# Moving GpSimd's arithmetic to VectorE and building RWKV's chunk inverses from 16x16 blocks

## The chip, the core and the metric

The kernel runs on one core of a Trainium2 chip. The core has a matrix engine (TensorE, PE in the profile, with its weight loads as PEld), a vector engine (VectorE, DVE), a scalar engine (ScalarE, ACT), a general engine (GpSimd, POOL) and a queue that issues transfers (SyncE, SP). Each engine executes its instructions strictly in the order in which they were placed in its stream; an instruction whose semaphores are not set holds up everything behind it on that engine. The metric is device time in microseconds of one launch.

## The reference

Two layers of a decoder over 512 tokens of 1024 channels. Each layer:

```python
h = modulate(rms_norm(x, norm1_g), shift1, scale1)
p = h @ w_in                      # columns for three mixers
y_ret, y_rwkv, y_conv = retention(p_ret), rwkv7_time_mix(p_rwkv), short_conv(p_conv)
merged = sum_i sigmoid(h @ w_gate + b_gate)_i * (y_i @ w_branch[i])
x = x + gate1 * (merged @ w_o)
h2 = modulate(rms_norm(x, norm2_g), shift2, scale2)
x = x + gate2 * hier_moe(h2)      # top-1 of 4 groups, then top-2 of its 8 experts
```

The part that matters most here is RWKV's recurrence, over 8 heads of 64:

```python
sk = einsum('bhvk,bhk->bhv', state, kht)
state = state * wt - sk[..., None] * (at * kht) + vt[..., None] * ktt
y = einsum('bhvk,bhk->bhv', state, rt)
```

## The kernel before

**Precision.** Projections are computed in float32 from fp32r parts. `split` (L216, L217) makes of a tile a high part on ScalarE and a low part, source minus high part, on VectorE or on the engine that the caller names. `wsplit` (L330) loads a weight block of 128 columns (`raw`) and splits it into `whi` and `wlo`, two buffers each; `mm3` (L345) then runs 24 matmuls per block: for each of 8 row blocks, `hTh` with `whi`, `hTl` with `whi` and `hTh` with `wlo`. In retention (`ret`), convolution (`conv`), part of the first norm and the first gates the caller names GpSimd for the low part. Five kinds of elementwise operation of the mixers are on GpSimd too, and so are the running sum of `merge` (L939) and the low parts of the routed tokens (L1048).

**Order.** The program is written as generators for RWKV, retention and convolution; a static scheduler interleaves them and fixes each engine's stream before the launch. RWKV runs in two halves (`rwkv_half`, two blocks of 128 channels, four heads each). Between its steps, projections of the other mixers stand on TensorE; retention's head norm (`head_norm`, with `rsqrt`, L206 to L211, and L582) gives `rB`, which L564 transposes; RWKV's gives `YN` for L884, and its key norm gives `rsq_y`, on which L701's matmul rests.

**The chunk inverse.** A chunk has 64 steps, and its state update needs the inverse of a 64x64 unit triangular matrix for each pair of head and chunk, 32 pairs in a half; even and odd chunks (`par`) lie on different halves of the partitions. `Lt` holds the strict parts, made on VectorE behind matmuls (L735, L739), and L764 uses them first. Each matrix has two diagonal 32x32 blocks (`ab`), so a half has 64 blocks of 32x32. Stores (L774) put them into DRAM (`nd`), and a load (L780) returns them with one block per partition (`P`). On VectorE, 31 steps of two operations (L786: outer product of a column of `P` with the rows found so far; L788: add into `T`) solve all 64 blocks at once on 64 partitions. `T` and its transpose go to DRAM (`td`, `ttd`) and come back into `tts`, which holds the transposed inverses in place, and `TA` (named `Ei` in the profile, whose buffer it uses). Then TensorE makes the off-diagonal 32x32 block: L806 multiplies the off-diagonal part of `Lt` with `TA`, ScalarE copies it (`Pb`, named `a`), and L811 multiplies with `tts`; ScalarE writes the result into `tts` (L813). This is done for the chunks of one parity and then for those of the other, 16 matmuls each time. L820 and what follows use `tts`.

**Routing.** After the second norm, tokens `x` are scaled by `r`. ScalarE makes `xr` (L1046) and the high part `xh` (L1047), GpSimd the low part of the first 768 channels (L1048); the last 256 channels' low parts (L1084) are made on VectorE in `late_xl`, behind the slot masks `oh` (L1080) of the first group in the program text. `route` finds groups and experts on VectorE (L1173 to L1195), counts places with matmuls (L1198, L1200), and L1203 makes the positions `pos`. `gather` multiplies `xh` and `xl` with `oh` (L1254), alternating between them over the four token blocks.

Of the kernel before, what the change touches and what calls it, by code (L numbers as in the profile page):

```python
# [37 lines left out]
def _consts():  # L38
# [136 lines left out]
class Kern:  # L175
# [44 lines left out]
    def setup(self):  # L220
# [139 lines left out]
    def norm1(self, l):  # L360
# [8 lines left out]
        if l == 0:  # L369
# [4 lines left out]
            ws = [self.wsplit(w_in(at), 8, nc.gpsimd if i % 2 else None, (self.wp, np_)[i // 2])  # L374
# [71 lines left out]
    def dense(self, l):  # L446
# [35 lines left out]
        self.merge(l, mg, [self.gate(l, mg, d, i, nc.gpsimd) for d, i in MERGE[:5]])  # L482
# [6 lines left out]
    def ret(self, l, pool, between):  # L489
        nc, c = self.nc, self.c  # L490
        b2 = lambda tag: pool.tile([128, S], F32, tag=tag, name=tag)
        def blk(o, h):
            ps = next(self.proj(l, "w_in", o * MW + h * 128, 1, nc.gpsimd))
            return ps

        A, B, C, Dt, E, F, G, H = "rA rB rC rD rE rF rG rH".split()
        for h in range(4):
            qk = []
            for o, tag in ((0, A), (1, B)):
# [7 lines left out]
                nc.gpsimd.tensor_tensor(t, t, self.sinT, op=OP.mult)  # L507
# [12 lines left out]
            nc.gpsimd.tensor_tensor(ch(qd), ch(q), c("decq")[:, None, h * 128:(h + 1) * 128].to_broadcast([128, 4, 128]),  # L520
# [121 lines left out]
    def rwkv_half(self, l, hf, rw, b2, half, wal, gl, wa, gd):  # L642
# [14 lines left out]
        for b in range(2):  # L657
# [30 lines left out]
            nc.gpsimd.tensor_scalar(a, a, 0.5, 0.5, op0=OP.mult, op1=OP.add)  # L688
# [81 lines left out]
        for par in range(2):  # L770
            for ab in range(2):
# [718 lines left out]
```

## Time and profile before

| what | us |
|---|---|
| plain runs, median of 3 | 2608.41 (2608.26 to 2610.09) |
| profiled execution | 2605.45, its span 2603.7 |
| mean granted TensorE clock | 0.966 of full |
| GpSimd: low parts of weights (L217) | 70 instructions, 170.2 |
| GpSimd: sums of the merge (L939) | 32, 53.4 |
| GpSimd: rotary products (L507) | 16, 21.9 |
| GpSimd: low parts of tokens (L1048) | 8, 14.8 |
| VectorE: inverse steps (L786, L788) | 248, 141.1 |

The times of one layer's stages, layer 0: first norm to 60 us, mixers 60 to 500, merge to 685, output projection and routing to 760, experts to 1300. Layer 1 follows the same pattern some 1304 us later.

How to read the rows: a timeline row gives start, duration, engine, line, operation, output and inputs by the program's names, and in brackets the idle time before it and what ended it. A row of waits gives engine, tile and line that waited, what it waited for, and then microseconds in total, number of times, longest. A row of groups gives the shapes and count, the busy time and the mean in ns, and the idle time before.

### The profile page before, as it was taken

Reading aid. Unit: us, or ns where it says so; the run is one execution under the profiler, and the core shown is the slowest. Engines: PE = TensorE matmul, PEld = TensorE weight load, DVE = VectorE, ACT = ScalarE, POOL = GpSimd, SP = SyncE. Lnnn points to the kernel's source line nnn. Section 1 sums busy time; section 2 is a strip of 40 time slices with the busy share of each in tenths; the row PEclk is TensorE's granted clock in tenths of the full one; section 3 lists DMA queues with packets and bytes.
Section 4 is the critical chain, followed back from the end, with each engine's and each line's share of the span. In section 5 each row is a group of like instructions: output and inputs, shape, how many; then the busy total and the mean of one; then the engine's idle time right before and its main releaser. Section 6 shows DMA issues by size and latency. Waiting matters only on the chain. (4 is left out here: it accounts for less than half of the span.)

```text
span 2603.7 us, 33403 instructions
## 1 busy us (share of the span) xinstructions
PE 2336.9 (90%) x13262; PEld 1559.8 (60%) x13262; DVE 1219.7 (47%) x2505; ACT 658.9 (25%) x1122; POOL 330.1 (13%) x200
## 2 busy tenths in 40 slices
PE   5988979899979999899989889798999799999997
PEld 4666667777854444444456666677789544444443
DVE  7677767676442223122246776676734422221223
ACT  4322323222331111111143222232233311111111
POOL 2132223211010000000011223232110100000000
PEclk9999989999989999999999999899999899999999
DMA  7131124575629997799842321255736299889993
GB/s 281 62 85 66 41 81 167 193 262 192 245 86 411 388 379 281 288 421 382 354 151 69 83 67 42 80 185 185 247 97 243 103 416 386 331 340 421 420 382 149
DMA packets 136610, 589.80 MB, mean 227 GB/s; under 512 B 34820, under 2 KB 35588, under 8 KB 87300
## 3 DMA queue, kind: packets, MB, share of 16 engines
q1 hardware_dynamic: 133280, 579.19, 58.7%
q10 hardware_dynamic: 3172, 8.45, 1.0%
q8 instruction: 106, 1.74, 0.3%
q14 instruction: 52, 0.43, 0.0%
HBM read 569.76 MB, written 13.63 MB: 224 GB/s over the span
## 5 line engine op out<-in xcount | busy, mean ns | idle before, releaser
L1273 PE MATMUL ps_mm<-w_at,xg_at 128*64 128x512 f32 x2048 | 470.4, 595 | 0.0
L345 PE MATMUL ps_mm<-hTh_at,wlo_at 128*128 128x512 f32 x1024 | 412.8, 403 | 38.3 <-POOL wlo_at L217 26.3
L345 PE MATMUL ps_mm<-hTh_at,whi_at 128*128 128x512 f32 x1024 | 414.8, 405 | 3.0 <-DVE wa_at L613 2.4
L345 PE MATMUL ps_mm<-hTl_at,whi_at 128*128 128x512 f32 x1024 | 410.8, 401 | 0.0
L1273 PEld LDWEIGHTS ps_mm<-w_at,xg_at 128*64 128x64 f32 x2048 | 155.6, 137 | 263.3 <-issue 258.3
L216 ACT ACTIVATE whi_at<-raw_at 128x1024 fp32r<-128x1024 f32 (+1 forms) x180 | 169.6, 944 | 449.1 <-PE ps_mm L345 303.3
L1305 PE MATMUL ps_rt<-w_at,hT_at 128*64 128x512 f32 x1024 | 268.3, 598 | 0.0
L1277 DVE TENSOR_TENSOR h_at<-h_at,ps_mm 128x256 f32<-128x256 f32 x65 | 27.4, 421 | 482.9 <-ACT h_at L1276 482.9
L345 PEld LDWEIGHTS ps_mm<-hTh_at,wlo_at 128*128 128x128 f32 x1024 | 197.0, 192 | 92.7 <-POOL wlo_at L217 29.7
L345 PEld LDWEIGHTS ps_mm<-hTh_at,whi_at 128*128 128x128 f32 x1024 | 197.1, 193 | 50.8 <-issue 7.6
L345 PEld LDWEIGHTS ps_mm<-hTl_at,whi_at 128*128 128x128 f32 x1024 | 197.1, 192 | 43.3 <-issue 3.2
L217 POOL TENSOR_TENSOR wlo_at<-raw_at,whi_at 128x1024 fp32r<-128x1024 f32 x70 | 170.2, 2435 | 391.2 <-ACT whi_at L216 339.4
L1305 PEld LDWEIGHTS ps_rt<-w_at,hT_at 128*64 128x64 f32 x1024 | 86.2, 136 | 136.4 <-issue 134.3
L217 DVE TENSOR_TENSOR wlo_at<-raw_at,whi_at 128x1024 fp32r<-128x1024 f32 (+1 forms) x110 | 115.4, 1050 | 105.8 <-ACT whi_at L216 105.5
L1311 DVE SCALAR_TENSOR_TENSOR ps_rt<-ps_rt,ws_at,g2b_at 128x512 f32<-128x512 f32 x66 | 50.1, 759 | 215.8 <-PE ps_rt L1305 212.6
L1254 PE MATMUL ps_sm<-oh_at,xh_at 128*128 128x256 f32 x512 | 131.4, 295 | 6.3 <-DVE oh_at L1080 2.4
L1276 ACT ACTIVATE h_at<-ps_mm 128x256 f32<-128x256 f32 x65 | 24.9, 383 | 440.6 <-PE ps_mm L1273 440.6
L1254 PE MATMUL ps_sm<-oh_at,xl_at 128*128 128x256 f32 x512 | 127.8, 289 | 0.0
L311 DVE SCALAR_TENSOR_TENSOR w_ada_at<-w_ada_at,crow_at 128x1024 f32<-128x1024 f32 x80 | 100.9, 1262 | 41.4 <-DMA w_ada_at<-in_w_ada_dram 41.2
L1329 DVE TENSOR_TENSOR x_at<-x_at,ps_sm 128x512 f32<-128x512 f32 x136 | 91.7, 687 | 55.1 <-PE ps_sm L1326 54.7
L1254 PEld LDWEIGHTS ps_sm<-oh_at,xh_at 128*128 128x128 f32 x512 | 100.3, 196 | 25.2 <-issue 25.2
L1326 PE MATMUL ps_sm<-yh_at,ohT_at 128*128 128x512 f32 x264 | 107.2, 410 | 5.2 <-ACT yh_at L1312 3.5
(364 smaller groups left out, 3404.3 us busy)
## 6 DMA issues: line engine op xcount, KB each, us to landing
w_at<-in_w_exp_dram SPq DMA_DIRECT2D x384, 1024.0 KB, 9.6
raw_at<-in_w_in_dram SPq DMA_DIRECT2D x84, 512.0 KB, 3.6
w_ada_at<-in_w_ada_dram SPq DMA_DIRECT2D x80, 512.0 KB, 4.3
raw_at<-in_w_gate_dram SPq DMA_DIRECT2D x48, 512.0 KB, 4.1
raw_at<-in_w_branch_dram SPq DMA_DIRECT2D x48, 256.0 KB, 3.9
w_ada_at<-in_w_ada_dram SPq DMA_DIRECT2D x8, 1024.0 KB, 12.8
raw_at<-in_w_o_dram SPq DMA_DIRECT2D x16, 512.0 KB, 4.4
yin_at<-yd SPq DMA_DIRECT2D x24, 256.0 KB, 3.3
```

The costliest lines, as they stand in the source:

```text
L216: nc.scalar.activation(hi, src, AF.Copy)
L217: (eng or nc.vector).tensor_tensor(lo, src, hi.bitcast(F32), op=OP.subtract)
L311: nc.vector.scalar_tensor_tensor(w, w, 1.0, self.crow, op0=OP.mult, op1=OP.mult, accum_out=m)
L345: self.nc.tensor.matmul(ps, w[a][:, k], x[b][:, k], start=n == 0, stop=n == last)
L1254: nc.tensor.matmul(po if len(oh.shape) == 4 else pg, src[:, t, k * 128:(k + 1) * 128], oh[:, t], start=i == 0, stop=i == 7)
L1273: nc.tensor.matmul(ph[64 * j:64 * j + 64].rearrange("p (u f) -> p u f", u=2), xg(k), wgu(k)[:, :, 256 * j:256 * j + 256], start=k == 0, st ...
L1276: nc.scalar.activation(h, ph[:, :256], AF.Silu)
L1277: nc.vector.tensor_tensor(h, h, ph[:, 256:], op=OP.mult)
L1305: nc.tensor.matmul(pys[n][64 * j:64 * j + 64], hT[j][:, f % 2, f // 2], wd(j, f)[:, 512 * n:512 * n + 512], start=f == 0, stop=f == 3)
L1311: nc.vector.scalar_tensor_tensor(y, y, ws, g2b[:, n * 512:(n + 1) * 512], op0=OP.mult, op1=OP.mult)
L1326: nc.tensor.matmul(px, ohT[:, t * 128:(t + 1) * 128], y, start=i == 0, stop=i == 2 * len(done) - 1)
L1329: nc.vector.tensor_tensor(xs, xs, px, op=OP.add)
```

## The change

1. **GpSimd's arithmetic.** Every elementwise operation that ran on GpSimd is issued on VectorE; GpSimd keeps the clearing of tiles.
2. **The chunk inverse.** The diagonal blocks that VectorE solves are 16x16: 128 blocks per half, one per partition, 15 steps of two operations in place of 31, on at most 64 elements instead of 256. DRAM goes by blocks of 16x16 (16 stores per half instead of 8, eight loads of `tts` instead of four and six of `TA` instead of two). Two 16x16 inverses are joined to a 32x32 one on TensorE: L807 multiplies `Lt`'s 32x32 diagonal block with the left half of `TA`; ScalarE copies the result with the rows of even 16-blocks set to zero (`odd16`) into `Pa`; L815 and L816 multiply with `tts`, for the straight and the transposed inverse, and VectorE (L820) and ScalarE put the results into `TA` and `tts`. The matmuls alternate between the four 32x32 diagonal tiles of the array. The join to 64x64 (now L827 and L836) alternates between the two parities matmul by matmul, and its copies are shared between VectorE and ScalarE.
3. **Token low parts.** `xr` is gone. All low parts of tokens are made in `late_xl` (L1113), eight of 512 channels, and `gather` takes the four `xh` before the four `xl`.

```diff
@@ wsplit's callers, ret, conv, gates, and the single operations, in this form: @@
-                nc.gpsimd.tensor_tensor(t, t, self.sinT, op=OP.mult)
+                nc.vector.tensor_tensor(t, t, self.sinT, op=OP.mult)
...
-                    nc.gpsimd.tensor_tensor(tot, tot, tg, op=OP.add)
+                    nc.vector.tensor_tensor(tot, tot, tg, op=OP.add)
...
-        for g in (32, 96):
-            nc.gpsimd.memset(self.tts[g:g + 32, :, :32], 0.0)
+        nc.gpsimd.memset(self.tts, 0.0)
...
         nd, td, ttd = self.nd[hf], self.td[hf], self.ttd[hf]
-        for par in range(2):
-            for ab in range(2):
-                p0 = (1 - par) * 64 + 32 * ab
-                for h in range(4):
-                    nc.sync.dma_start(nd[par, ab, 4 * h:4 * h + 4].rearrange("c s t -> s c t"),
-                                      Lt[p0:p0 + 32, h, par::2, 32 * ab:32 * ab + 32])
+        quarters = [(par, ab, (1 - par) * 64 + 32 * ab) for par in range(2) for ab in range(2)]
+        for b in range(2):
+            for par, ab, p0 in quarters:
+                for q in range(2):
+                    nc.sync.dma_start(nd[par, ab, q, 8 * b:8 * b + 8].rearrange("(h c) s t -> s h c t", h=2),
+                                      Lt[p0 + 16 * q:p0 + 16 * q + 16, 2 * b:2 * b + 2, par::2,
+                                         32 * ab + 16 * q:32 * ab + 16 * q + 16])
         pt_ = rw["pt"]
-        P = pt_.tile([64, 32, 32], F32, tag="P", name="P")
-        T = pt_.tile([64, 32, 32], F32, tag="T", name="T")
-        tmp = pt_.tile([64, 32 * 32], F32, tag="tmp", name="tmp")
-        nc.sync.dma_start(P, nd.rearrange("a b n s t -> (a b n) s t"))
+        P, T, TT, tmp = (pt_.tile([128, 16, 16], F32, tag=n, name=n) for n in ("P", "T", "TT", "tmp"))
+        tmp = tmp.rearrange("p a b -> p (a b)")
+        nc.sync.dma_start(P, nd.rearrange("a b q n s t -> (a b q n) s t"))
         nc.gpsimd.memset(T, 0.0)
-        nc.gpsimd.memset(T.rearrange("p t s -> p (t s)")[:, ::33], 1.0)
-        for j in range(31):
-            n, m = 31 - j, j + 1
+        nc.gpsimd.memset(T.rearrange("p t s -> p (t s)")[:, ::17], 1.0)
+        for j in range(15):
+            n, m = 15 - j, j + 1
             tv = tmp[:, :n * m].rearrange("p (i s) -> p i s", s=m)
-            nc.vector.tensor_tensor(tv, P[:, j, j + 1:][:, :, None].to_broadcast([64, n, m]),
-                                    T[:, j, :m][:, None, :].to_broadcast([64, n, m]), op=OP.mult)
+            nc.vector.tensor_tensor(tv, P[:, j, j + 1:][:, :, None].to_broadcast([128, n, m]),
+                                    T[:, j, :m][:, None, :].to_broadcast([128, n, m]), op=OP.mult)
             nc.vector.tensor_tensor(T[:, j + 1:, :m], T[:, j + 1:, :m], tv, op=OP.add)
-        TT = pt_.tile([64, 32, 32], F32, tag="P", name="TT")
         nc.vector.tensor_copy(TT, T.rearrange("p t s -> p s t"))
-        nc.sync.dma_start(td.rearrange("a b n t s -> (a b n) t s"), T)
-        nc.sync.dma_start(ttd.rearrange("a b n s t -> (a b n) s t"), TT)
+        nc.sync.dma_start(td.rearrange("a b q n t s -> (a b q n) t s"), T)
+        nc.sync.dma_start(ttd.rearrange("a b q n s t -> (a b q n) s t"), TT)
         TA = b2("Ei").rearrange("p (n s) -> p n s", s=32)
-        for par in range(2):
-            for ab in range(2):
-                p0 = (1 - par) * 64 + 32 * ab
-                nc.sync.dma_start(tts[p0:p0 + 32, :, 32 * ab:32 * ab + 32], ttd[par, ab].rearrange("n s t -> s n t"))
-            p0 = (1 - par) * 64
-            nc.sync.dma_start(TA[p0:p0 + 32], td[par, 0].rearrange("n t s -> t n s"))
+        nc.gpsimd.memset(TA, 0.0)
+        for par, ab, p0 in quarters:
+            for q in range(2):
+                at = slice(p0 + 16 * q, p0 + 16 * q + 16)
+                nc.sync.dma_start(tts[at, :, 32 * ab + 16 * q:32 * ab + 16 * q + 16],
+                                  ttd[par, ab, q].rearrange("n s t -> s n t"))
+                if not (ab and q):
+                    nc.sync.dma_start(TA[at, :, 16 * q:16 * q + 16], td[par, ab, q].rearrange("n t s -> t n s"))
+
+        Pa = pt_.tile([128, 16, 16], F32, tag="Pa", name="Pa")
+        pp = self.psum()[:, :256].rearrange("p (n s) -> p n s", s=16)
+        for n in range(16):
+            for par, ab, p0 in quarters:
+                at = slice(p0, p0 + 32)
+                nc.tensor.matmul(pp[at, n], Lt[at, n // 4, 2 * (n % 4) + par, 32 * ab:32 * ab + 32], TA[at, n, :16],
+                                 start=True, stop=True, tile_position=(p0, p0))
+        nc.scalar.activation(Pa, pp, AF.Copy, scale=c("odd16"))
+        px, pq = (z.rearrange("p (n s) -> p n s", s=16) for z in (lambda t: (t[:, :256], t[:, 256:]))(self.psum()))
+        for n in range(16):
+            for par, ab, p0 in quarters:
+                at = slice(p0, p0 + 32)
+                if not ab:
+                    nc.tensor.matmul(px[at, n], tts[at, n, :32], Pa[at, n], start=True, stop=True, tile_position=(p0, p0))
+                nc.tensor.matmul(pq[p0:p0 + 16, n], Pa[at, n], tts[at, n, 32 * ab + 16:32 * ab + 32], start=True, stop=True,
+                                 tile_position=(p0, p0))
+        for par, ab, p0 in quarters:
+            if not ab:
+                nc.vector.tensor_tensor(TA[p0:p0 + 32, :, :16], TA[p0:p0 + 32, :, :16], px[p0:p0 + 32], op=OP.add)
+            nc.scalar.activation(tts[p0:p0 + 16, :, 32 * ab + 16:32 * ab + 32], pq[p0:p0 + 16], AF.Copy)
         Pb = b2("a").rearrange("p (n s) -> p n s", s=32)
-        for par in range(2):
-            a0 = (1 - par) * 64
-            b0 = a0 + 32
-            pp = self.psum().rearrange("p (n s) -> p n s", s=32)
-            for n in range(16):
+        pp, pq = (self.psum().rearrange("p (n s) -> p n s", s=32) for _ in range(2))
+        sides = [(par, (1 - par) * 64, (1 - par) * 64 + 32) for par in range(2)]
+        for n in range(16):
+            for par, a0, b0 in sides:
                 nc.tensor.matmul(pp[b0:b0 + 32, n], Lt[a0:a0 + 32, n // 4, 2 * (n % 4) + par, 32:], TA[a0:a0 + 32, n],
                                  start=True, stop=True, tile_position=(a0, b0))
-            nc.scalar.activation(Pb[b0:b0 + 32], pp[b0:b0 + 32], AF.Copy)
-            pq = self.psum().rearrange("p (n s) -> p n s", s=32)
-            for n in range(16):
+        for par, a0, b0 in sides:
+            if par:
+                nc.vector.tensor_copy(Pb[b0:b0 + 32], pp[b0:b0 + 32])
+            else:
+                nc.scalar.activation(Pb[b0:b0 + 32], pp[b0:b0 + 32], AF.Copy)
+        for n in range(16):
+            for par, a0, b0 in sides:
                 nc.tensor.matmul(pq[a0:a0 + 32, n], Pb[b0:b0 + 32, n], tts[b0:b0 + 32, n, 32:], start=True, stop=True,
                                  tile_position=(b0, a0))
-            nc.scalar.activation(tts[a0:a0 + 32, :, 32:], pq[a0:a0 + 32], AF.Copy)
+        for par, a0, b0 in sides:
+            if par:
+                nc.vector.tensor_copy(tts[a0:a0 + 32, :, 32:], pq[a0:a0 + 32])
+            else:
+                nc.scalar.activation(tts[a0:a0 + 32, :, 32:], pq[a0:a0 + 32], AF.Copy)
 
...
-        xs, cut = self.area(SB_XG, 2), D - 256
         for t in range(NT):
-            xr = xs.tile([128, D], F32, tag="xr", name="xr")
-            nc.scalar.activation(xr, x[:, t], AF.Copy, scale=r[:, t:t + 1])
             nc.scalar.activation(xh[:, t], x[:, t], AF.Copy, scale=r[:, t:t + 1])
-            nc.gpsimd.tensor_tensor(xl[:, t, :cut], xr[:, :cut], xh[:, t, :cut].bitcast(F32), op=OP.subtract)
...
-        late_xl = lambda: [nc.vector.scalar_tensor_tensor(xl[:, t, cut:], x[:, t, cut:], r[:, t:t + 1],
-                                                          xh[:, t, cut:].bitcast(F32), op0=OP.mult, op1=OP.subtract)
-                           for t in range(NT)]
+        def late_xl():
+            for w in range(2):
+                ws = slice(w * 512, w * 512 + 512)
+                for t in range(NT):
+                    nc.vector.scalar_tensor_tensor(xl[:, t, ws], x[:, t, ws], r[:, t:t + 1], xh[:, t, ws].bitcast(F32),
+                                                   op0=OP.mult, op1=OP.subtract)
+
...
-            for t in range(NT):
-                for src in (xh, xl):
+            for src in (xh, xl):
+                for t in range(NT):
                     nc.tensor.matmul(po if len(oh.shape) == 4 else pg, src[:, t, k * 128:(k + 1) * 128], oh[:, t], start=i == 0, stop=i == 7)
```

The scheduler places the new program's instructions anew; line numbers behind the changed places move on (L217 is now L218, L345 L346, L613 L614).

On VectorE, within the first half of layer 0, this stood around the longest steps of the inverse; the names are those of the text above:

```order
L613 SCALAR_TENSOR_TENSOR rkv_at_408<-ps_mm,cv_at_63,rkv_at_408 128x511
L788 TENSOR_TENSOR T_at_850<-T_at_850,tmp_at_851 64x21x11
L786 TENSOR_TENSOR tmp_at_851<-P_at_849,T_at_850 64x240
L788 TENSOR_TENSOR T_at_850<-T_at_850,tmp_at_851 64x20x12
L786 TENSOR_TENSOR tmp_at_851<-P_at_849,T_at_850 64x247
L788 TENSOR_TENSOR T_at_850<-T_at_850,tmp_at_851 64x19x13
L786 TENSOR_TENSOR tmp_at_851<-P_at_849,T_at_850 64x252
L788 TENSOR_TENSOR T_at_850<-T_at_850,tmp_at_851 64x18x14
```

and this stands there now, the low parts of weights (L218) and the mixing of shifted projections (L614) among shorter steps:

```order
L788 TENSOR_TENSOR T_at_849<-T_at_849,tmp_at_851 128x7x9
L786 TENSOR_TENSOR tmp_at_851<-P_at_848,T_at_849 128x60
L788 TENSOR_TENSOR T_at_849<-T_at_849,tmp_at_851 128x6x10
L218 TENSOR_TENSOR wlo_at_111<-raw_at_106,whi_at_109 128x1024
L786 TENSOR_TENSOR tmp_at_851<-P_at_848,T_at_849 128x55
L614 SCALAR_TENSOR_TENSOR rkv_at_407<-ps_mm,cv_at_63,rkv_at_407 128x511
L788 TENSOR_TENSOR T_at_849<-T_at_849,tmp_at_851 128x5x11
L786 TENSOR_TENSOR tmp_at_851<-P_at_848,T_at_849 128x48
```

The low part was in GpSimd's stream and is now between two steps of the inverse, and the steps have 128 partitions in place of 64.

On TensorE, the first join of the same half stood behind 165 projection matmuls since the last L764:

```order
L345 MATMUL ps_mm<-hTl_at_85,whi_at_108 128x512
L345 MATMUL ps_mm<-hTh_at_84,wlo_at_110 128x512
L345 MATMUL ps_mm<-hTh_at_84,whi_at_108 128x512
L806 MATMUL ps_sm<-Ei_at_553,Lt_at_402 32x32 x16
L345 MATMUL ps_mm<-hTl_at_85,whi_at_108 128x512
L345 MATMUL ps_mm<-hTh_at_84,wlo_at_110 128x512
L525 MATMUL ps_rt<-consts_at_61,rD_at_2313 128x128 x4
```

Now the first products of the 16x16 blocks stand behind 129 projection matmuls since the last L764 (three single ones of the 64 are placed earlier among them), and three projection matmuls lie between them and the next step:

```order
L346 MATMUL ps_mm<-hTh_at_84,whi_at_109 128x512
L346 MATMUL ps_mm<-hTl_at_85,whi_at_109 128x512
L346 MATMUL ps_mm<-hTh_at_84,wlo_at_111 128x512
L807 MATMUL ps_sm<-Ei_at_552,Lt_at_401 32x16 x61
L346 MATMUL ps_mm<-hTh_at_84,whi_at_109 128x512
L346 MATMUL ps_mm<-hTl_at_85,whi_at_109 128x512
L346 MATMUL ps_mm<-hTh_at_84,wlo_at_111 128x512
L815 MATMUL ps_sm<-Pa_at_903,tts_at_399 32x16
L816 MATMUL ps_sm<-tts_at_399,Pa_at_903 16x16 x2
```

The place moved 36 projection matmuls ahead. The further steps (L827, L836) follow with three to five projection matmuls between each two.

On VectorE, at the routing of layer 0, this stood ahead of the positions:

```order
L1178 TENSOR_REDUCE r_at_5407<-r_at_5384 128x16
L1084 SCALAR_TENSOR_TENSOR xl_at_5375<-x_at_60,rsq_y_at_5357,xh_at_5374 128x256
L1179 TENSOR_TENSOR r_at_5384<-consts_at_61,r_at_5407 128x128
L1194 TENSOR_TENSOR r_at_5384<-r_at_5384,r_at_5386 128x128
L1195 TENSOR_TENSOR r_at_5385<-r_at_5383,r_at_5384 128x128
L1084 SCALAR_TENSOR_TENSOR xl_at_5375<-x_at_60,rsq_y_at_5357,xh_at_5374 128x256
L1203 SCALAR_TENSOR_TENSOR pos_at_5418<-ps_sm,r_at_5385 128x128
```

and now

```order
L1204 TENSOR_TENSOR r_at_5673<-r_at_5671,r_at_5692 128x128
L1113 SCALAR_TENSOR_TENSOR xl_at_5664<-x_at_60,rsq_y_at_5646,xh_at_5663 128x512
L1205 TENSOR_TENSOR r_at_5673<-r_at_5673,consts_at_61 128x128
L1113 SCALAR_TENSOR_TENSOR xl_at_5664<-x_at_60,rsq_y_at_5646,xh_at_5663 128x512
L1207 TENSOR_REDUCE r_at_5696<-r_at_5673 128x16
L1237 TENSOR_TENSOR r_at_5846<-lg_at_5665,r_at_5685 128x16
```

followed by the rest of the routing, with L1224 (L1195 before) and L1232 (L1203 before) four and ten rows behind the last one shown. All eight low parts of 512 channels stand ahead of the positions; two of the four of 256 channels stood ahead of L1195 before, and a third between L1195 and L1203.

More of the change, by code (lines that the diff above doesn't have):

```diff
@@ L57, in _consts @@
     parts["same"] = same * 1.0
+    parts["odd16"] = (p // 16 % 2 * 1.0)[:, None]
     parts["sel2"] = (p[:, None] // 64 == np.arange(2)[None, :]) * 1.0
@@ L237, in setup @@
         self.yd = [dram([MW, S], "yd%d" % i) for i in range(3)]
-        self.nd = [dram([2, 2, 16, 32, 32], "nd%d" % i) for i in range(2)]
-        self.td = [dram([2, 2, 16, 32, 32], "td%d" % i) for i in range(2)]
-        self.ttd = [dram([2, 2, 16, 32, 32], "ttd%d" % i) for i in range(2)]
+        self.nd = [dram([2, 2, 2, 16, 16, 16], "nd%d" % i) for i in range(2)]
+        self.td = [dram([2, 2, 2, 16, 16, 16], "td%d" % i) for i in range(2)]
+        self.ttd = [dram([2, 2, 2, 16, 16, 16], "ttd%d" % i) for i in range(2)]
     def x_src(self, l):
@@ L373, in norm1 @@
                 nc.sync.dma_start(x[:, t], self.x_src(0)[t * 128:(t + 1) * 128])
-            ws = [self.wsplit(w_in(at), 8, nc.gpsimd if i % 2 else None, (self.wp, np_)[i // 2])
+            ws = [self.wsplit(w_in(at), 8, None, (self.wp, np_)[i // 2])
                   for i, at in enumerate(first)]
@@ L384, in norm1 @@
             for at in first[:2]:
-                self.early["w_in", l, at] = self.wsplit(w_in(at), 8, nc.gpsimd)
+                self.early["w_in", l, at] = self.wsplit(w_in(at), 8)
         r = self.inv_rms(np_, ss, NT)
@@ L405, in parts @@
                 nc.scalar.activation(h, h, AF.Identity, bias=b[:, k:k + 1])
-                nc.gpsimd.tensor_tensor(hT[1][:, k], h, hT[0][:, k].bitcast(F32), op=OP.subtract)
+                nc.vector.tensor_tensor(hT[1][:, k], h, hT[0][:, k].bitcast(F32), op=OP.subtract)
             else:
@@ L481, in dense @@
         mg = self.area(SB_GATES, 6)
-        self.merge(l, mg, [self.gate(l, mg, d, i, nc.gpsimd) for d, i in MERGE[:5]])
+        self.merge(l, mg, [self.gate(l, mg, d, i) for d, i in MERGE[:5]])
     def put(self, i, b, y):
@@ L492, in blk @@
         def blk(o, h):
-            ps = next(self.proj(l, "w_in", o * MW + h * 128, 1, nc.gpsimd))
+            ps = next(self.proj(l, "w_in", o * MW + h * 128, 1))
             return ps
@@ L587, in blk @@
         def blk(o, b):
-            ps = next(self.proj(l, "w_in", CONV0 + o * MW + b * 128, 1, nc.gpsimd))
+            ps = next(self.proj(l, "w_in", CONV0 + o * MW + b * 128, 1))
             return ps
@@ L687, in rwkv_half @@
             nc.vector.tensor_tensor(kt, k, kt, op=OP.mult)
-            nc.gpsimd.tensor_scalar(a, a, 0.5, 0.5, op0=OP.mult, op1=OP.add)
+            nc.vector.tensor_scalar(a, a, 0.5, 0.5, op0=OP.mult, op1=OP.add)
             kk = b2("kk")
```

10 lines of the change are left out of this document (5 added, 5 removed).

## The prediction

> **What bounds the kernel now.** I read the head of the page first, then the table by stretches of time (60–500: the mixers of layer 0; 760–1300: its experts; 1364–1804: the mixers of layer 1), then the table of waits of TensorE within 60–500.
>
> ```profile
> span 2603.7 us, 33403 instructions
> PE 2336.9 (90%) x13262; PEld 1559.8 (60%) x13262; DVE 1219.7 (47%) x2505; ACT 658.9 (25%) x1122; POOL 330.1 (13%) x200
> ```
> ```profile
> core 0: us, PE busy (x) PEld busy (x) DVE busy (x) ACT busy (x) POOL busy (x), PEclk, DMA share, GB/s
> 60.00:500.00 440.00, 382.31 (x2689) 298.82 (x2687) 298.06 (x611) 130.46 (x196) 118.98 (x71) 0.94 0.30 93
> 760.00:1300.00 540.00, 509.16 (x2535) 254.68 (x2536) 126.14 (x284) 93.54 (x186) 1.03 (x2) 0.99 0.89 357
> 1364.00:1804.00 440.00, 383.42 (x2703) 299.77 (x2702) 290.82 (x601) 127.83 (x190) 118.55 (x69) 0.94 0.31 95
> ```
> ```profile
> PE ps_mm L345 <- POOL wlo_at L217: 13.9, 4, 8.2
> PE ps_rt L564 <- DVE rB_at L582: 11.4, 2, 7.5
> PE ps_sm L701 <- DVE rsq_y_at L211: 10.5, 3, 5.1
> PE ps_sm L884 <- DVE YN_at L582: 6.8, 2, 5.2
> PE ps_sm L806 <- DMA Ei_at<-td: 6.1, 2, 4.6
> ```
>
> TensorE is busy for 90% of the span; what can be won is its idle time and its slow clock. The experts have a busy TensorE, clock 0.99 and no GpSimd work to speak of (1.03 us), so the change leaves them alone. Each mixer stage has 440 − 382 = 58 us of idle TensorE, and a clock of 0.94, that is 0.06 × 440 = 26 us lost at half speed. The waits of 60–500 come to 57 us; the five quoted make 48.7 of it. Every one of the five ends on a low part made by GpSimd, on a chain of VectorE, or on the inverse's loads. Neither engine is full: VectorE works 298 of 440 us, GpSimd 119. So these are latencies, and the next view asks what stretches them.
>
> ```profile
> L217 POOL TENSOR_TENSOR wlo_at<-raw_at,whi_at 128x1024 fp32r<-128x1024 f32 x33 | 80.1, 2432 | 185.0 <-ACT whi_at L216 166.5 <-PE ps_mm L345 18.4
> L217 DVE TENSOR_TENSOR wlo_at<-raw_at,whi_at 128x1024 fp32r<-128x1024 f32 x62 | 75.8, 1224 | 101.7 <-ACT whi_at L216 101.4 <-DMA w_ada_at<-in_w_ada_dram 0.3
> ```
> ```profile
> 150.35 2.39 POOL L217 TENSOR_TENSOR wlo_at<-raw_at,whi_at 128x1024 fp32r<-128x1024 f32 x1 [2.99 <-ACT whi_at L216]
> ```
> ```profile
> 150.09 0.37 DVE L786 TENSOR_TENSOR tmp_at<-P_at,T_at 64x207 f32<-64x207 f32 x1
> 150.49 2.49 DVE L788 TENSOR_TENSOR T_at<-T_at,tmp_at 64x207 f32<-64x207 f32 x1
> ```
> ```profile
> 235.58 2.26 DVE L209 TENSOR_TENSOR rsq_s_at<-rsq_y_at 128x8 f32<-128x8 f32 x1
> 237.88 0.17 DVE L210 TENSOR_TENSOR rsq_s_at<-rsq_s_at,rsq_x_at 128x8 f32<-128x8 f32 x1
> ```
>
> Within 60–500 a low part takes 2.43 us on GpSimd and, by the group over the whole run, 1.22 on VectorE. While GpSimd works, a VectorE operation of 0.4 us takes 2.49 and one of 0.17 takes 2.26: it is held until GpSimd ends. Such holds sit in the chains that TensorE waits for.
>
> **The change, part by part.** All sums are made against the profiled execution's 2605.45 us; the median of the plain runs, 2608.41, lies 3 us above it.
>
> *Low parts.* Per mixer stage 33 subtractions leave GpSimd: 80 us there become 33 × 1.22 = 40 us on VectorE; the smaller moved operations, some 25 of 0.2 to 0.7, I put at 15 us. VectorE has 142 us idle and gets back its holds. How large these are the inverse shows:
>
> ```profile
> L788 DVE TENSOR_TENSOR T_at<-T_at,tmp_at 64x31 f32<-64x31 f32 (+15 forms) x124 | 70.6, 569 | 3.3
> L786 DVE TENSOR_TENSOR tmp_at<-P_at,T_at 64x31 f32<-64x31 f32 (+15 forms) x124 | 70.5, 569 | 6.5 <-DMA P_at<-nd 3.5
> ```
> ```profile
> 141.49 0.18 DVE L786 TENSOR_TENSOR tmp_at<-P_at,T_at 64x31 f32<-64x31 f32 x1 [1.28 <-DMA P_at<-nd]
> 141.71 0.21 DVE L788 TENSOR_TENSOR T_at<-T_at,tmp_at 64x31 f32<-64x31 f32 x1
> ...
> 183.65 0.18 DVE L788 TENSOR_TENSOR T_at<-T_at,tmp_at 64x31 f32<-64x31 f32 x1
> ```
>
> Their mean of 569 ns stands against 0.18 to 0.37 in the undisturbed rows, so about 0.2 us × 248 = 50 us of holding in these lines alone.
>
> *Inverse.* Before: 62 steps, 141.49 to 183.83, 42 us. After: 30 steps of 15 to 64 elements on 128 partitions; the first two rows follow each other by 0.22 us, so 6.6 us, plus some 5 us of three low parts and two evacuations that the new order puts between them. On SP's queue 16 stores go ahead in place of 8, and 14 loads come behind in place of 6, at 0.46 us each (3.65 / 8):
>
> ```profile
> 132.93 3.65 SPq L774 DMA_DIRECT2D nd<-Lt_at  x8
> ```
> ```profile
> 188.03 1.90 SPq L797 DMA_DIRECT2D tts_at<-ttd  x4
> ```
>
> So P comes 3.7 us later and the steps start at 145; they end near 157; between the last step and the first L797 lie 4.2 us today, so the loads start near 161, and 14 × 0.47 us later, at 167.6, the last is issued; it lands near 169. TensorE's side: the order before put 165 projection matmuls between L764 and L806, now 129 stand between L764 and the last 61 of L807. At 0.227 us each
>
> ```profile
> 228.58 0.39 PE L345 MATMUL ps_mm<-hTh_at,wlo_at 128*128 128x512 f32 x1
> 228.81 0.39 PE L345 MATMUL ps_mm<-hTh_at,whi_at 128*128 128x512 f32 x1
> ```
>
> that is 37.5 and 29.3 us; 188.82 less its wait of 1.51, the 8.2 us low-part wait and 37.5 puts the end of L764 at 141.6, so TensorE is there at 171. The margin is some 2 us, no more than its error, and each load is queued behind the one ahead on SP. The wait for Ei, 6.1 us a stage (two halves), I put at 2; bounds 0 and 6.6, the whole row of loads in one half.
>
> *New matmuls.* 160 per half, two passes each: 320.
>
> ```profile
> 188.82 1.17 PE L806 MATMUL ps_sm<-Ei_at,Lt_at 32*32 32x32 f32 x32 [1.51 <-DMA Ei_at<-td]
> ...
> 208.44 2.09 PE L848 MATMUL ps_sm<-WV_at,X_at 128*64 128x64 f32 x64
> ```
>
> On one tile of the array 32 columns cost 1.17 / 32 = 37 ns with the tail of the last, some 32 without. L848, alternating between two tiles, has 64 columns at 2.09 / 64 = 33 ns, so two tiles work side by side. The new matmuls alternate between four tiles, and the old join now between two. Bounds per half: nothing (8 ns each, less what the old 128 passes save) to 320 × 32 ns = 10 us. I take 4, nearest to L848's halved price, 8 a layer.
>
> [...]
>
> ```profile
> 202.32 3.38 PE L820 MATMUL ps_sm<-WV_at,tts_at 64*64 64x128 f32 x55
> ```
>
> 3.38 / 55 = 61 ns for 128 columns is half of L806's price per column: pairs do overlap in one bank.
>
> *Routing.* Here the first slots wait on a chain of VectorE (layer 1 likewise):
>
> ```profile
> 755.89 0.77 PE L1198 MATMUL ps_sm<-r_at,consts_at 128*128 128x128 f32 x2 [14.20 <-DVE r_at L1195]
> ```
> ```profile
> 746.02 2.04 DVE L1084 SCALAR_TENSOR_TENSOR xl_at<-x_at,rsq_y_at,xh_at 128x256 fp32r<-128x256 f32 x1
> 747.98 0.28 DVE L1179 TENSOR_TENSOR r_at<-consts_at,r_at 128x128 f32<-128x128 f32 x1
> 748.30 1.78 DVE L1189 SCALAR_TENSOR_TENSOR r_at<-r_at,r_at 128x128 f32<-128x128 f32 x1
> ```
>
> Four such operations are held by about 1.5 us each (2.04 and 1.78 are two of them): 6 us go. But the new order places eight low parts of 512 columns ahead of the positions (L1232), at half of 1.22 us and a little, 0.65 each, in place of two of 256 columns at some 0.4: 4 us come back. That is −2 a layer, and half a us of clock; bounds −6 (the low parts fall into waits) and +1. ScalarE's four copies that go lie beside this chain and are worth nothing. The gather's first four matmuls take the high parts alone, so a late low part is covered by them.
>
> *Merge and first norm.* The 16 sums of L939 per layer go to VectorE, which TensorE waits for there already, over the run
>
> ```profile
> PE ps_mm L345 <- DVE wlo_at L217: 12.6, 18, 1.2
> ```
>
> 0.7 us a time. A sum of 512 columns (0.65 us) lies beside 24 matmuls, 5.4 us; all 16 on the path would be +10 a layer, the holds gone −2; taken −1, since the cover is eight times the cost. The first norm of layer 0 is a chain on VectorE:
>
> ```profile
> 34.78 2.29 DVE L299 SCALAR_TENSOR_TENSOR w_ada_at<-w_ada_at,crow_at 128x1024 f32<-128x1024 f32 x1
> ```
>
> held for 1.1 us against 1.22 for the same size, in three of four steps, against four added subtractions that lie partly behind ScalarE: −1.5 (bounds −3 and +3).
>
> *What stays of the mixers' waits.* Low parts 13.9 → 4 (six at 0.7); rB 11.4 → 3.5 and YN 6.8 → 2, since holds go, while about as many projections cover them (at the second head 48 stood between its sums and L564 and 7.5 us were missing, a chain of 48 × 0.227 + 7.5 = 18.4 us; 42 or 9.5 us stand there now, against a chain that loses its holds and the long steps that alternate with its rsq); rsq_y 10.5 → 4.5; Ei 2; the rest 8.3 → 6. That is 57 → 22, −35 a layer. The slow clock goes with such waits: the second L806 of the layer, right behind its wait of 4.6, took twice the first's time.
>
> ```profile
> 360.89 1.91 PE L806 MATMUL ps_sm<-Ei_at,Lt_at 32*32 32x32 f32 x32 [4.56 <-DMA Ei_at<-td]
> ```
>
> Of 26 us of lost clock I take back 12, a little under the share of the waits that goes (35 of 57 would be 16), since the longest that stay keep theirs.
>
> Layer 0: −35 − 12 + 8 − 2.5 − 1 − 1.5 = −44; layer 1 without the norm −42.5. Sum −86.5: 2519 for a profiled run, 3 more for the median: **2522**.
>
> **Rivals.** (a) *VectorE's queue becomes the wait.* Each low part waits there for ScalarE, which waits for a free buffer, that is for TensorE; everything behind it (rsq, the TA sum, evacuations) waits too. For it: 101.4 us of such waiting in the group of 62 above. Against: VectorE's idle third. At the merge's 0.7 us for each of 33: +23 a layer, 2568. (b) *The small matmuls run one at a time,* at 32 ns: +6 per half, +24, 2546. The pairing of L848 speaks against it; untried is 16 columns.
>
> [...]
>
> (c) *Slower:* (a) with its full price. If each of the 66 low parts reaches TensorE later than today by 2.4 us, one GpSimd duration, because a wait ahead of it in the queue is unmet, that is 158 us: 2680. It turns the sign from 86.5 / 66 = 1.3 us. Against: the part itself is 1.2 us shorter. (d) *The waits only change names* (14 loads, ScalarE's copies, PSUM): 2600 ± 10.
>
> **How the numbers follow.** Forecast 0.58; (a) 0.18; (b) 0.11; (c) 0.05; (d) 0.08, half within 0.2% (about what a measurement of this kernel can tell from no change), half faster. Faster 0.91, same 0.04, slower 0.05. Low end: waits down to 8 (−49), clock −22, matmuls +1, the rest −5: −75 a layer, 2458. High end: half the waits stay (−28), clock −6, matmuls +20, nothing else: −14 a layer, 2580, which takes in (a) and (b). Outside lie (c), (d) and the forecast's own tails.
>
> **What would show it.** Right: no GpSimd row but memsets; steps of the inverse near 7 us of work, no VectorE row of 0.2 us at 2; TensorE's waits in 60–500 near 22 us, clock 0.97; L807 starting without a wait; L807 to L816 with starts 12 ns apart. Wrong: waits for wlo on VectorE above 15 us a layer; L807 waiting on Ei's or tts's loads; starts 25 to 32 ns apart; a routing gap still of 14 us.

## The result and the profile after

The changed kernel takes 2497.4 us (median of 4, 2493.6 to 2502.7) against 2609.1 (4 runs): a ratio of 0.957, 95% interval 0.956 to 0.959. The profiled execution took 2497.34 us, 108.1 less than that of before. The forecast was 2522, and the time lies inside its range of 2458 to 2580.

The head of the page of the changed kernel:

```profile
span 2495.6 us, 35836 instructions
PE 2324.4 (93%) x14542; PEld 1553.7 (62%) x14542; DVE 1123.7 (45%) x2569; ACT 657.8 (26%) x1126; POOL 7.4 (0%) x26
```

GpSimd is left with its clearing of tiles (7.4 us), and VectorE, which took its work over, is busy for 96 us less than before. The new program orders the merge's first projections among the mixers' last, so the fair stretch to compare is from the first projection to the first matmul of the output projection (L1009 before, L1038 after). Two tables of stretches, before and after, layer 0, with the columns of the prediction's:

```profile
63.30:678.30 615.00, 549.76 (x3414) 432.74 (x3414) 417.17 (x809) 178.11 (x260) 145.34 (x85) 0.96 0.41 134
```
```profile
61.00:621.60 560.60, 542.93 (x4054) 429.45 (x4054) 366.31 (x827) 180.95 (x266) 2.54 (x9) 0.98 0.45 145
```

The stretch is 54.4 us shorter: TensorE's idle time falls from 65.2 to 17.7 us (−47.5), its busy time by 6.8 although it has more matmuls, since the loss to the slow clock went from 0.04 × 615 = 25 to 0.02 × 561 = 11 us (the clocks are read to two digits, so each product is good to some 3 us). Over the whole run TensorE's idle time (span less busy time) falls by 95.6 us, twice that of this stretch. What TensorE still waits for there, from the table of waits:

```profile
PE ps_mm L346 <- DVE wlo_at L218: 5.5, 10, 0.9
PE ps_sm L816 <- issue: 4.4, 3, 2.1
PE ps_mm L346 <- DVE b_at L964: 2.9, 2, 2.3
PE ps_mm L346 <- DVE wa_at L614: 2.8, 1, 2.8
...
PE ps_rt L565 <- DVE rB_at L583: 0.3, 1, 0.3
```

rB, 11.4 us before, is 0.3; YN and Ei are gone from the table. A new name is "issue" inside the joins. The long rows of VectorE are gone too: among rows whose line and shape take under 0.3 us at their shortest, the longest was 2.33 us before and is 0.30 now. VectorE's timeline shows the inverse of the first half:

```profile
138.25 0.17 DVE L786 TENSOR_TENSOR tmp_at<-P_at,T_at 128x15 f32<-128x15 f32 x1 [2.78 <-DMA P_at<-nd]
...
140.78 1.23 DVE L218 TENSOR_TENSOR wlo_at<-raw_at,whi_at 128x1024 fp32r<-128x1024 f32 x1 [1.91 <-ACT whi_at L217]
141.92 0.18 DVE L788 TENSOR_TENSOR T_at<-T_at,tmp_at 128x28 f32<-128x28 f32 x1
...
150.36 0.17 DVE L788 TENSOR_TENSOR T_at<-T_at,tmp_at 128x15 f32<-128x15 f32 x1
```

The 30 steps end after 12.3 us, with low parts between them: one makes the step behind it, whose product was ready at 138.87 us, wait with it for ScalarE, 1.91 us. This is rival (a) at work, but in time that was free, as TensorE's timeline shows. It has the joins:

```profile
166.12 1.21 PE L807 MATMUL ps_sm<-Ei_at,Lt_at 32*32 32x16 f32 x122
...
169.82 0.19 PE L816 MATMUL ps_sm<-tts_at,Pa_at 32*16 32x16 f32 x2 [1.18 <-issue]
```

L807 starts without a wait, 10 ns a pass, and within L816 TensorE stands for 1.18 us on nothing that the profile's waits name. At the routing the wait is 2.1 us shorter:

```profile
698.10 0.77 PE L1227 MATMUL ps_sm<-r_at,consts_at 128*128 128x128 f32 x2 [12.11 <-DVE r_at L1240]
```

### The profile page after: what moved, and what is told of

The parts are those of the page before. It is cut to its first block, busy times and chain, and to the rows that moved or that the text cites. A ratio compares the mean times of both kernels' runs of the same rounds, so it can differ in the third digit from the quotient of the medians.

```text
span 2495.6 us, 35836 instructions
## 1 busy us (share of the span) xinstructions
PE 2324.4 (93%) x14542; PEld 1553.7 (62%) x14542; DVE 1123.7 (45%) x2569; ACT 657.8 (26%) x1126; POOL 7.4 (0%) x26
## 5 line engine op out<-in xcount | busy, mean ns | idle before, releaser
L346 PE MATMUL ps_mm<-hTh_at,whi_at 128*128 128x512 f32 x1024 | 412.8, 403 | 8.1 <-DVE wa_at L614 3.6
L346 PE MATMUL ps_mm<-hTh_at,wlo_at 128*128 128x512 f32 x1024 | 409.1, 399 | 9.2 <-DVE wlo_at L218 9.2
L346 PE MATMUL ps_mm<-hTl_at,whi_at 128*128 128x512 f32 x1024 | 408.2, 399 | 0.0
L217 ACT ACTIVATE whi_at<-raw_at 128x1024 fp32r<-128x1024 f32 (+1 forms) x180 | 170.1, 946 | 468.4 <-PE ps_mm L346 379.9
L218 DVE TENSOR_TENSOR wlo_at<-raw_at,whi_at 128x1024 fp32r<-128x1024 f32 (+1 forms) x180 | 194.0, 1080 | 170.7 <-ACT whi_at L217 160.1
L346 PEld LDWEIGHTS ps_mm<-hTh_at,wlo_at 128*128 128x128 f32 x1024 | 194.8, 190 | 60.5 <-DVE wlo_at L218 17.1
L346 PEld LDWEIGHTS ps_mm<-hTh_at,whi_at 128*128 128x128 f32 x1024 | 195.0, 190 | 51.6 <-ACT whi_at L217 6.2
L346 PEld LDWEIGHTS ps_mm<-hTl_at,whi_at 128*128 128x128 f32 x1024 | 195.2, 191 | 41.6 <-issue 2.4
L1341 ACT ACTIVATE yh_at<-ps_rt 128x512 fp32r<-128x512 f32 x66 | 39.5, 598 | 263.3 <-DVE ps_rt L1340 263.3
L1355 PE MATMUL ps_sm<-yl_at,ohT_at 128*128 128x512 f32 x264 | 102.4, 394 | 0.6 <-DVE yl_at L1342 0.6
L1285 ACT ACTIVATE xg_at<-ps_sm,mod_at,mod_a_at 128x256 f32<-128x256 f32 x136 | 76.9, 565 | 87.5 <-PE ps_sm L1283 86.5
L1283 PE MATMUL ps_sm<-oh_at,xh_at 128*128 128x256 f32 x512 | 90.3, 297 | 6.6 <-DVE oh_at L1105 2.9
```

The costliest lines, as they stand in the source:

```text
L217: nc.scalar.activation(hi, src, AF.Copy)
L218: (eng or nc.vector).tensor_tensor(lo, src, hi.bitcast(F32), op=OP.subtract)
L346: self.nc.tensor.matmul(ps, w[a][:, k], x[b][:, k], start=n == 0, stop=n == last)
L1283: nc.tensor.matmul(po if len(oh.shape) == 4 else pg, src[:, t, k * 128:(k + 1) * 128], oh[:, t], start=i == 0, stop=i == 7)
L1285: nc.scalar.activation(xg[:, k], pg, AF.Identity, scale=a[:, k:k + 1], bias=b[:, k:k + 1])
L1341: nc.scalar.activation(yh, y, AF.Copy)
```

## The experiments

**Which part brings it.** Each of the three parts was applied alone to the kernel before; the parts are those of the diff above.

Part 1 alone, in this form at every place but the token low parts:

```diff
-                nc.gpsimd.tensor_tensor(t, t, self.sinT, op=OP.mult)
+                nc.vector.tensor_tensor(t, t, self.sinT, op=OP.mult)
```

> Part 1 alone: GpSimd's arithmetic on VectorE, but the old 32x32 inverse and the old token low parts. If holding by GpSimd and its longer low parts are what stretched the chains (my account): most of the gain, 2525 to 2550 us, TensorE's waits in the first mixer stage (57 us before, 11 after the whole change) near 20. If the old inverse's 62 long steps were the main cost (rival): 2570 or more, with the waits for rB, YN and Ei still there. If VectorE's queue, now with the long steps and the low parts together, becomes the wait: above 2590.

Part 2 alone, from the new blocks to the new joins:

```diff
-        for j in range(31):
+        for j in range(15):
...
+        Pa = pt_.tile([128, 16, 16], F32, tag="Pa", name="Pa")
```

> Part 2 alone: the 16x16 inverse, GpSimd keeps its arithmetic. My account: the inverse's own waits (Ei, 6 us a layer) and part of those for rB and YN go, the joins cost 18 us over the run, and holds stay: 2580 to 2600 us. Rival (the inverse is the main cost): 2540 or less.

Part 3 alone:

```diff
-            nc.gpsimd.tensor_tensor(xl[:, t, :cut], xr[:, :cut], xh[:, t, :cut].bitcast(F32), op=OP.subtract)
...
-            for t in range(NT):
-                for src in (xh, xl):
+            for src in (xh, xl):
+                for t in range(NT):
```

> Part 3 alone: token low parts on VectorE, the high parts first in the gather. Only the routing is touched: the wait before the counting matmuls goes from 14.2 to about 12 us a layer, 2604 us; no stage before it moves.

Part 1 alone takes 2478.1 us (ratio 0.949, 0.947 to 0.951): it gains more than the whole change, and more than was expected of it. Part 2 alone takes 2608.0 (0.999, 0.998 to 1.001), above its expected range, and part 3 alone 2607.3 (0.999, 0.997 to 1.001): neither can be told from nothing. So with GpSimd out of the way parts 2 and 3 together cost 19 us; the runs on the joins below put this on the new inverse. The waits with part 1 alone, same stretch:

```profile
PE ps_mm L345 <- DVE wlo_at L217: 9.3, 13, 2.3
...
PE ps_sm L884 <- DVE YN_at L582: 2.4, 2, 2.2
...
PE ps_rt L564 <- DVE rB_at L582: 1.0, 2, 0.7
```

Ei does not appear among the nine rows: the old 62 steps come in time when nothing holds them. Their groups say so, part 1 alone:

```profile
L788 DVE TENSOR_TENSOR T_at<-T_at,tmp_at 64x31 f32<-64x31 f32 (+15 forms) x124 | 41.2, 332 | 2.5
L786 DVE TENSOR_TENSOR tmp_at<-P_at,T_at 64x31 f32<-64x31 f32 (+15 forms) x124 | 41.0, 331 | 9.5 <-DMA P_at<-nd 7.1
```

569 ns has become 332, without a change to the steps themselves: their busy time falls from 141 to 82 us, so 59 us had been holds. With part 2 alone the new steps, on fewer elements, have means of 277 and 384 ns, against 206 and 203 in the changed kernel, and TensorE's waits for rB and rsq_y are still 10.5 and 13.8 us in layer 0.

**Which of GpSimd's operations.** One run puts the low parts of weights back on GpSimd in the changed kernel, one moves nothing but them in the kernel before.

Weights back, on the changed kernel, likewise in `conv` and the first gates:

```diff
-            ps = next(self.proj(l, "w_in", o * MW + h * 128, 1))
+            ps = next(self.proj(l, "w_in", o * MW + h * 128, 1, nc.gpsimd))
```

> The whole change, but the 33 low parts of weights of each mixer stage go back to GpSimd. If these are the cause (2.4 us each, and VectorE held meanwhile): 2540 to 2570 us, with rows of 0.2 us at 2 on VectorE again and TensorE waiting on wlo from GpSimd. If the short operations that moved were as important: 2505 to 2520.

Only the weights, on the kernel before, likewise in `conv`, the first norm and the gates:

```diff
-            ps = next(self.proj(l, "w_in", o * MW + h * 128, 1, nc.gpsimd))
+            ps = next(self.proj(l, "w_in", o * MW + h * 128, 1))
```

> Of part 1 only the low parts of weights (70 subtractions of 128x1024) go to VectorE; the short operations of the mixers, the sums of the merge and the token low parts stay on GpSimd, old inverse. All of part 1 gave 2478 us. If the weights are nearly all of it, as putting them back suggested (92 of 112 us): 2490 to 2505. If the short operations hold VectorE as much per microsecond of GpSimd (some 35 us in each mixer stage and 27 in each merge remain): 2510 to 2540.

Back on GpSimd they make 2589.0 us (0.992, 0.991 to 0.994): 92 of the 112 us are lost again, beyond what was expected. Moved alone they make 2513.1 (0.964, 0.960 to 0.967), and the remaining operations of part 1 another 35. This is the second of the two cases expected: the shorter operations hold VectorE as well, and with them on GpSimd the old steps of L788 still take 393 ns instead of 332. The first run's waits show where TensorE stands:

```profile
PE ps_rt L565 <- DVE rB_at L583: 11.1, 3, 5.4
PE ps_sm L815 <- issue: 7.2, 2, 3.8
...
PE ps_sm L913 <- DVE YN_at L583: 6.1, 2, 4.1
...
PE ps_mm L346 <- POOL wlo_at L218: 0.3, 1, 0.3
```

TensorE hardly waits for GpSimd's low parts themselves. It waits for chains on VectorE, as before the change, and longer on "issue" in the joins.

**Is it the hold, or the work's place?** Here the whole changed program stays, and GpSimd gets work on the side: behind each of 28 weight blocks a layer it either subtracts the two tiles once more into a scratch tile, or reads 8 columns and then only clears. The order of instructions on TensorE, VectorE, ScalarE and SyncE is unchanged.

Added behind `wsplit`'s `split`, first the reads, then the writes:

```diff
+    for i in range(4):
+        self.nc.gpsimd.tensor_tensor(self.scr, raw[:, 2 * i:2 * i + 2], hi[:, 2 * i:2 * i + 2].bitcast(F32), op=OP.subtract)
```
```diff
+    self.nc.gpsimd.tensor_tensor(self.scr[:, 0, :8], raw[:, 0, :8], hi[:, 0, :8].bitcast(F32), op=OP.subtract)
+    for i in range(9):
+        self.nc.gpsimd.memset(self.scr, 0.0)
```

> The whole change, and behind the 28 weight blocks of retention and convolution of each layer GpSimd also subtracts the same two tiles, into a scratch tile that nobody reads (four instructions of 128x256, about 0.6 us each). The order on the four other engines is the same, instruction by instruction, and nobody waits for GpSimd. If VectorE is held while GpSimd reads, VectorE's rows lengthen again and the time rises by 10 to 50 us, 2510 to 2550. If what counted was only that GpSimd took 2.4 us for a part that TensorE waits for (rival), the time stays at 2497 within 4.

> As the run with the added subtractions, but behind each block GpSimd reads only 8 columns and then clears the scratch tile nine times, about the same time busy. If reading holds VectorE: 2497 within 4, and no long rows. If any work of GpSimd holds it: as much longer as with the subtractions.

With the subtractions 2558.4 us, 61 more than the changed kernel (0.981 of before, 0.978 to 0.984); with the clears 2503.1 (0.959, 0.957 to 0.962), whose interval overlaps the changed kernel's, 0.956 to 0.959. The groups of both, GpSimd's and then the inverse's, with one of TensorE's waits from layer 0; first the reads:

```profile
L1523 POOL TENSOR_TENSOR scr_at<-raw_at,whi_at 128x256 f32<-128x256 f32 x224 | 222.5, 993 | 350.2 <-issue 286.9 <-ACT whi_at L217 49.6 <-POOL scr_at L1523 0.8
...
L788 DVE TENSOR_TENSOR T_at<-T_at,tmp_at 128x15 f32<-128x15 f32 (+7 forms) x60 | 22.2, 370 | 1.2
...
PE ps_rt L565 <- DVE rB_at L583: 10.2, 3, 4.1
```

and the writes:

```profile
L1524 POOL MEMSET scr_at<- 128x256 f32 x504 | 157.6, 313 | 28.8
L1522 POOL TENSOR_TENSOR scr_at<-raw_at,whi_at 128x8 f32<-128x8 f32 x56 | 44.2, 789 | 300.0 <-issue 243.1 <-ACT whi_at L217 49.5 <-POOL scr_at L1524 7.4
...
L788 DVE TENSOR_TENSOR T_at<-T_at,tmp_at 128x15 f32<-128x15 f32 (+7 forms) x60 | 12.4, 206 | 1.2
...
PE ps_rt L565 <- DVE rB_at L583: 0.5, 1, 0.5
```

and the same steps in the changed kernel:

```profile
L788 DVE TENSOR_TENSOR T_at<-T_at,tmp_at 128x15 f32<-128x15 f32 (+7 forms) x60 | 12.3, 206 | 1.2
```

GpSimd is busy for 222 and 202 us; the same steps of VectorE take 370 ns beside its subtractions and 206 beside its clears, and 206 in the changed kernel. TensorE's wait for rB, 0.3 us in the changed kernel, is 10.2 beside the subtractions and 0.5 beside the clears. So it is not GpSimd's being busy that counts in these runs, but its reading. One thing in the expectations was wrong: ScalarE does wait for GpSimd, since it may not overwrite the high part before it is read. That holds for both runs, 25 us of such waits for the subtractions and 42 for the clears, so it does not account for the 55 us between them. The runs leave open why putting the weights back costs 92 us, with 161 us of GpSimd, and the added subtractions only 61, with 222.

**The price of the joins.** Three runs. In the first the joins go through one tile of the array after the other.

```diff
-        for n in range(16):
-            for par, ab, p0 in quarters:
+        for par, ab, p0 in quarters:
+            for n in range(16):
```

> The whole change, but the matmuls of the joins go through one 32x32 tile after the other in place of alternating. If the four tiles work side by side in the change: L807 goes from 9 ns a pass to about 32, 20 us more over the run by 640 passes at 23 ns and the wider joins 8 more: 2520 to 2525 us. If one at a time is no dearer, 2497. The idle times of 1 to 2 us within the joins, which end on nothing that the profile shows, should go if they come from issuing faster than instructions arrive.

It takes 2551.2 us (0.978, 0.976 to 0.980), 54 more than the change, about twice what was expected. Two of its rows of TensorE:

```profile
160.79 1.18 PE L807 MATMUL ps_sm<-Ei_at,Lt_at 32*32 32x16 f32 x32
...
177.60 1.91 PE L827 MATMUL ps_sm<-Ei_at,Lt_at 32*32 32x32 f32 x32
```

On one tile 16 columns cost as much as 32 did (1.18 us for 32 passes, against 1.17 in the prediction's row). So alternating is what makes the change bearable: 10 ns a pass instead of 37. The second row is at half the clock (0.50 granted from 175 to 180 us), and the stretch of 165 to 210 us shows where the rest comes from, in this run and then with part 1 alone. TensorE is fully busy in both:

```profile
165.00:210.00 45.00, 45.00 (x632) 36.59 (x629) 16.62 (x29) 9.30 (x17) 0.00 (x0) 0.70 0.12 34
```
```profile
165.00:210.00 45.00, 45.00 (x503) 37.03 (x501) 29.73 (x72) 15.32 (x23) 0.12 (x1) 1.00 0.31 92
```

TensorE never idles there, yet the granted clock falls to 0.70 while the joins run on one tile, and to 0.50 in the 20 us from 175 on; the changed kernel has 0.92 in that stretch. The idle times within the joins are gone, at the same number of instructions issued more slowly. That instructions arrive too late for passes 10 ns apart is my estimate of the cause, made from this run and from the changed kernel's trace. There the queue that the profile's page names "instruction" moves packets of 16 KB, three of them between 167 and 175 us, where the first joins run:

```profile
q8 instruction: 3, 0.05, 2.9%
```

Each of the six idle times within the joins that end on "issue", 9.7 us over the run, ends 1.2 to 1.6 us after such a packet has landed. The packets do not say for which engine they are and no run changed them, so this cause is not shown.

The other two runs separate the first joins from the last one:

The changed kernel without L807, L815, L816 and what copies their results, so that the off-diagonal 16x16 blocks stay zero; the edit goes from the first to the last of these lines:

```diff
-        Pa = pt_.tile([128, 16, 16], F32, tag="Pa", name="Pa")
...
-            nc.scalar.activation(tts[p0:p0 + 16, :, 32 * ab + 16:32 * ab + 32], pq[p0:p0 + 16], AF.Copy)
```

> The whole change without the joins of 16x16 blocks (their three groups of matmuls and the operations that copy the results are left out, so the off-diagonal 16x16 blocks stay zero); the 15 short steps, the 14 loads and the last join stay. If part 2 loses only by these matmuls (26.6 us of TensorE over the run, idle times within them included, and the half-clock time behind them): 2465 to 2472, about that of the old inverse with the alternating last join, and then the shorter steps on VectorE are worth nothing by themselves. If the shorter steps gain: below 2462. If the 14 loads or stores cost: 2480 or more.

Part 1 alone, and of part 2 only the order and the shared copies of the last join:

```diff
-            for n in range(16):
+        for n in range(16):
+            for par, a0, b0 in sides:
```

> GpSimd's arithmetic moved and the old 32x32 inverse kept (2478 us in its own run), and of the new inverse only the last join: the 32x32 products alternate between the two parities and their copies are shared by two engines. These products took 17.6 us of TensorE over the run one at a time and 10.6 alternating: 2469 to 2474 us if the price of the joins is what matters, 2478 if they lie beside something.

Without the 16x16 joins: 2465.1 us (0.944, 0.942 to 0.947). With the old inverse and the alternating last join: 2465.7 (0.945, 0.943 to 0.947). The two agree. So what only the first of them has, the shorter steps with their 14 loads and 16 stores and part 3, is together worth nothing that can be told from noise. The first joins cost 2497.4 − 2465.1 = 32 us, and the alternating last join, the same in both, gains 2478.1 − 2465.7 = 12 (the intervals, 0.947 to 0.951 and 0.943 to 0.947, just meet), a little more than expected. Of these 12 its matmuls account for 7: 17.6 us of TensorE became 10.4. Where the other 5 come from was not traced.

**The routing, and the best of it.** In the changed kernel the low parts are tied to the positions:

```diff
+            r2 = ms_.tile([128, NT], F32, name="rx")
+            nc.vector.scalar_tensor_tensor(r2, pos[:, :, 0], 0.0, r, op0=OP.mult, op1=OP.add)
...
-                    nc.vector.scalar_tensor_tensor(xl[:, t, ws], x[:, t, ws], r[:, t:t + 1], xh[:, t, ws].bitcast(F32),
+                    nc.vector.scalar_tensor_tensor(xl[:, t, ws], x[:, t, ws], r2[:, t:t + 1], xh[:, t, ws].bitcast(F32),
```

> The whole change, but the token low parts depend on the positions (their scale is added to zero times a position), so that all eight stand behind them on VectorE. If they lengthen the chain before the counting matmuls: the wait of 12.1 us a layer goes to about 8, and part of it comes back as a wait of the gather for low parts; 2490 to 2496. If the chain is bound otherwise: 2497.

And the old 32x32 inverse with part 1, part 3, the alternating last join and this `r2`:

> GpSimd's arithmetic moved, old inverse with the alternating last join, and the token low parts on VectorE behind the positions, high parts first in the gather. Sum of the parts: 7 us from the join and 4 to 6 from the routing off 2478: 2463 to 2470 us. If the parts take the same wait: 2472 to 2478.

With the low parts behind the positions the wait falls to 7.5 us a layer:

```profile
695.38 0.76 PE L1229 MATMUL ps_sm<-r_at,consts_at 128*128 128x128 f32 x2 [7.48 <-DVE r_at L1226]
```

and the time to 2493.4 us (0.956, 0.954 to 0.958), 4 less than the change, whose interval it overlaps; 9 us of wait went over two layers, and the time shows less than half. All of the good parts together take 2455.5 us (0.941, 0.939 to 0.944), 42 less than the change, with intervals apart, and better than the sum of the parts that was expected. This version beats both kernels.

## Why the prediction was right, and where it was not

*Direction and mechanism.* Both were right. The gain comes from the mixers, by the holds that GpSimd's reading puts on VectorE's chains; the added subtractions show it without any other change of order (370 ns a step of L788, against 206 beside the clears). Rivals (c) and (d) are out by the time itself.

*The waits that stay* are the mis-sized term. For mixers and merge the forecast was −35 − 1 a layer; the idle time fell by 47.5 in layer 0. The 11.5 more, twice, are 23 us, about what the forecast is too high by (25). Of rB, rsq_y, YN and Ei I kept 12 of 35 us a layer, and 2 are left: of the chain that took 18.4 us at the second head no wait above 0.3 us remains.

*The clock*: 12 us a layer were forecast, and some 13 were measured in that stretch. One of its readings was off: the second L806, 1.91 us against the first's 1.17, took 1.6 times the time, not twice; the granted clock was 0.50 from 360 to 365 us and 0.91 and 0.90 in the 5 us before and after. That the slow clock goes with waits holds for that row; the joins on one tile had 0.70 over 45 us without one.

*The inverse* was put in the wrong column. Its step "the wait for Ei, 6.1 us a stage, I put at 2" gave to shorter steps what the end of the holds does by itself: with part 1 alone, and so with the old steps, Ei is not waited for either. Part 1 alone is 19 us faster than the whole change. The timetable was off as well: the steps start at 138.25 us and not at 145, since eight of the 16 stores were issued at 105 us and only the other eight at 130.

*The new matmuls.* 16 us were forecast; the time from their starts to the next matmul's, summed over the joins, went from 18.9 to 37.2 us, so 18 more. That the size is right is partly luck: the passes run at 10 ns, near the low bound, but idle times within them and slow clock behind them (0.56 of full from 170 to 175 us, 0.75 from 175 to 180) were not in the sum, so that the first joins cost 32 us, and the alternating last join gave 12 us back, more than assumed. Rival (b) is out: 122 passes on four tiles that all write one `ps_sm` tile take 1.21 us, 10 ns a pass. No run shows starts 25 ns apart, the lower end of what the forecast named as its sign of being wrong; measured were 10 ns with four tiles in turn and 37 with one.

*Rival (a)* happens in part: VectorE waits 160 us for ScalarE's high parts in its low-part rows, 105 before, but TensorE waits for low parts only 9.2 us over the whole run; the rival's price was 46.

*Routing*: the wait is 2.1 us shorter, 2 were forecast, and part 3 alone shows the same 12.1 us. But it is given back: from the first matmul of the output projection to the first of the experts it is 85 us in layer 0 before and after (763.3 − 678.4, 706.7 − 621.7), and part 3 alone is within noise. *Norm*: its end moved from 63.4 to 61.1 us, 2.3 against the 1.5 forecast.

## What to carry to other kernels

An engine that is a quarter busy, as GpSimd was in the mixers (119 of 440 us), can be the bottleneck through another one's rows: when rows of one length show one that is six times longer, here 2.49 us against 0.4, look at what runs beside them before shortening them. Test such a suspicion by adding the suspected work, unused, to the fast version. And time each part of a change alone, since here the part that looked most like work saved was the one that cost.

## What the runs showed of the hardware that was not expected

TensorE lost its clock while it was busy without a gap: with the joins on one 32x32 tile it was busy for 45.00 of 45 us and the granted clock fell to 0.70; with part 1 alone, where whole-array projections ran between shorter bursts, it was as busy over the same stretch, at 1.00. Why is not shown. A 16-column pass on one tile took the same 37 ns (1.18 us for 32) as a 32-column one (1.17), while four tiles in turn gave 10 ns (1.21 us for 122). And the short passes in series of the changed kernel's joins leave idle times of 1 to 2 us that no wait of the profile explains, 4.4 us in layer 0; all six of the run, 9.7 us, end 1.2 to 1.6 us after a packet of the instruction queue has landed.
